# Row sizes of the last stores and the first loads where a streaming kernel goes from one half of its tokens to the next

## The chip, the core and the metric

The kernel runs on one core of a Trainium2 chip. The core has five engines with instruction streams of their own, and 16 DMA engines that carry data between the core's on-chip memory (SBUF, 128 partitions) and the device memory (HBM). The metric is the device time of one execution in microseconds (us). Before the change it is 242.05 us, the median of eight executions between 241.79 and 242.74 us.

## The reference

For each of 16 x 1024 tokens there is a row of 512 fp32 numbers and eight router logits. The two largest softmax weights, made to sum to one, scale two copies of the token's row:

```python
probs = softmax(router_logits)                       # (16, 1024, 8)
topk_indices = np.argsort(probs, axis=-1)[..., -k:]  # k = 2
topk_probs = np.take_along_axis(probs, topk_indices, axis=-1)
topk_probs = topk_probs / np.sum(topk_probs, axis=-1, keepdims=True)
return x[:, :, None, :].repeat(k, axis=2) * topk_probs[..., None]
```

The input is 33.6 MB and the output 67.1 MB. There are no matrix products. With two weights that sum to one, each of them is a sigmoid of the difference of the two largest logits.

## The kernel before

The 16384 tokens are laid over the 128 partitions, 128 consecutive tokens to each. A token is 2 KB of input and 4 KB of output, so in HBM a partition owns 256 KB of consecutive input and 512 KB of consecutive output. One DMA moves n tokens of every partition; it is cut into 128 rows, one per partition, and a row is n x 2 KB for a load and n x 4 KB for a store. Each row is one packet, and each of the 16 DMA engines carries eight of the 128.

First the logits are loaded (L72) and `top2_weights` works out `WA`, both weights of all tokens, on VectorE (DVE) and ScalarE (ACT). Then two groups of 64 tokens per partition follow (`GROUP = 64`, `M = 128`).

Two buffers hold the work. `xs` has room for the 64 input tokens of a group, 128 KB in each partition. `osp` has room for 16 output tokens, 64 KB. One DVE instruction (L99) multiplies n input tokens by their two weights and writes 2n rows. Which tokens go where is written out by hand in `plan`: tokens 0 to 15 go to `osp`, in pieces of 2 and 14. Tokens 16 to 31 go to `low`, the first half of `xs`, whose own input has been used by then. Tokens 32 to 47 go to `osp` again, in two pieces of 8. Tokens 48 to 63 go to `high`, the second half of `xs`, in two pieces of 8. Each piece is stored right after it is made (L107). So the second group's loads of tokens 0 to 31 must wait for the store from `low`, and its loads of 32 to 47 and of 48 to 63 for the first and the second store from `high`.

SP (SyncE) issues every DMA but one: the first store of the first group goes out on ACT's queue. SP issues in program order, and an issue that must wait holds back the later ones. The order is: logits, four loads of 16 tokens, the first group's stores, the second group's four loads (L96), the second group's stores. Once issued, the transfers of a queue are carried in the order of issue by each DMA engine. Eight completion semaphores are given out to the DMAs in turn, and an issue also waits until the DMA that had its semaphore before has landed.

Of the kernel before, what the change touches and what calls it, by code (L numbers as in the profile page):

```python
# [1 line left out]

# [4 lines left out]

F32 = mybir.dt.float32
ALU = mybir.AluOpType
ACTF = mybir.ActivationFunctionType  # L10
P = 128


def top2_weights(nc, pool, logits, M, E):

    hi, lo, n = None, None, E
    while n > 1:  # L20
        n //= 2
        if hi is None:
            a, b = logits[:, :, 0:n], logits[:, :, n : 2 * n]
            nhi = pool.tile([P, M, n], F32, tag=f"hi{n}")
            nlo = pool.tile([P, M, n], F32, tag=f"lo{n}")
            nc.vector.tensor_tensor(nhi, a, b, op=ALU.max)  # L26
            nc.vector.tensor_tensor(nlo, a, b, op=ALU.min)  # L27
        else:
            a, b = hi[:, :, 0:n], hi[:, :, n : 2 * n]
            nhi = pool.tile([P, M, n], F32, tag=f"hi{n}")  # L30
            nlo = pool.tile([P, M, n], F32, tag=f"lo{n}")
            tmp = pool.tile([P, M, n], F32, tag=f"tmp{n}")
            nc.vector.tensor_tensor(tmp, lo[:, :, 0:n], lo[:, :, n : 2 * n], op=ALU.max)  # L33
            nc.vector.tensor_tensor(nlo, a, b, op=ALU.min)  # L34
            nc.vector.tensor_tensor(nlo, nlo, tmp, op=ALU.max)  # L35
            nc.vector.tensor_tensor(nhi, a, b, op=ALU.max)  # L36
        hi, lo = nhi, nlo
    dlt = pool.tile([P, M], F32, tag="dlt")
    nc.vector.tensor_tensor(dlt, hi[:, :, 0], lo[:, :, 0], op=ALU.subtract)  # L39
    WA = pool.tile([P, M, 2], F32, tag="WA")  # L40
    nc.scalar.activation(WA[:, :, 0], dlt, ACTF.Sigmoid, scale=-1.0)  # L41
    nc.scalar.activation(WA[:, :, 1], dlt, ACTF.Sigmoid, scale=1.0)  # L42
    return WA


@with_exitstack
def kernel(
    ctx: ExitStack,
    tc: tile.TileContext,
    x: bass.AP,  # L50
    router_logits: bass.AP,
    k: bass.AP,
    out: bass.AP,
):
    nc = tc.nc
    B, S, D = x.shape
    E = router_logits.shape[-1]
    N = B * S
    assert int(k) == 2 and E == 8 and N % P == 0
    M = N // P  # L60

    GROUP = 64
    L = 16
    x_v = x.rearrange("b s d -> (b s) d").rearrange("(p m) d -> p m d", p=P)
    o_v = out.rearrange("b s k d -> (b s) k d").rearrange("(p m) k d -> p m k d", p=P)
    rl_v = router_logits.rearrange("b s e -> (b s) e").rearrange(
        "(p m) e -> p m e", p=P
    )

    wpool = ctx.enter_context(tc.tile_pool(name="wpool", bufs=1))  # L70
    logits = wpool.tile([P, M, E], F32)
    nc.sync.dma_start(logits, rl_v)  # L72
    WA = top2_weights(nc, wpool, logits, M, E)

    xs = wpool.tile([P, GROUP, D], F32)
    osp = wpool.tile([P, L, 2, D], F32)


    low = xs[:, : 2 * L, :].rearrange("p (r k) d -> p r k d", k=2)
    high = xs[:, 2 * L :, :].rearrange("p (r k) d -> p r k d", k=2)  # L80
    h = L // 2
    e = 2
    plan = [
        (0, e, osp[:, :e]),
        (e, L - e, osp[:, e:]),
        (L, L, low),
        (2 * L, h, osp[:, :h]),
        (2 * L + h, h, osp[:, h:]),
        (3 * L, h, high[:, :h]),
        (3 * L + h, h, high[:, h:]),  # L90
    ]

    for g in range(M // GROUP):
        m0 = g * GROUP
        for r in range(0, GROUP, L):
            nc.sync.dma_start(xs[:, r : r + L, :], x_v[:, m0 + r : m0 + r + L, :])  # L96
        for r, n, og in plan:
            rows = slice(m0 + r, m0 + r + n)
            nc.vector.tensor_tensor(  # L99
                og,  # L100
                xs[:, r : r + n, :].unsqueeze(2).to_broadcast([P, n, 2, D]),
                WA[:, rows, :].unsqueeze(3).to_broadcast([P, n, 2, D]),
                op=ALU.mult,
            )

            queue = nc.scalar if rows.start == 0 else nc.sync
            queue.dma_start(o_v[:, rows], og)  # L107


# [1 line left out]
_INS = ['x', 'router_logits', 'k']  # L111
_OUTS = [((16, 1024, 2, 512), 'float32')]

_NUMBERS = {'k': 2}


# [26 lines left out]
```

## Time and profile before

| | us |
|---|---|
| median of eight executions (lowest, highest) | 242.05 (241.79, 242.74) |
| the profiled execution, device time | 242.65 |
| its span on the core | 240.9 |
| outside its span | 1.75 |
| busy DVE | 142.1 |
| busy ACT | 1.8 |
| share of 16 DMA engines' span in use, SP's queue and ACT's | 97.5% and 1.0% |
| mean rate of the DMA engines | 420 GB/s |

The span runs from the first to the last instruction of the core. "Busy" of the DMA engines is the time that their packets took; a packet that is held up counts in full, so that a share near 100% can still hide lost time, and the rate must be read with it. The trace also holds the start, the duration and the size of each packet. The packets of one DMA engine follow each other without a gap, so the engine that carried a packet can be told from the ends and starts.

### The profile page before, as it was taken

How to read it: one execution, taken by the hardware profiler on the slowest of the kernel's cores; microseconds unless marked ns; L12 is line 12 of the kernel's file. 1: busy time of each engine (PE TensorE's matmuls, PEld its weight loads, DVE VectorE, ACT ScalarE, POOL GpSimd, SP SyncE). 2: the span in 40 equal slices, each digit the busy share in tenths (PEclk: the TensorE clock that was granted, in tenths of full speed). 3: DMA queues.
4: the chain of work that ended last, by engine and by line, in shares of the span. 5: the costliest groups of instructions: out<-in, count | busy, mean ns of one | idle time of the engine just before them, and what ended most of it. 6: DMA issues, size and time to landing. Idle time of an engine off the chain costs nothing.

```text
span 240.9 us, 116 instructions
## 1 busy us (share of the span) xinstructions
DVE 142.1 (59%) x25; ACT 1.8 (1%) x3; POOL 0.2 (0%) x4
## 2 busy tenths in 40 slices
DVE  2369999900499999200000999997007999990000
ACT  2000000000000000000000000000000000000000
POOL 0000000000000000000000000000000000000000
DMA  7999999997999999999999999999999999999995
GB/s 261 435 435 392 457 452 435 484 438 324 501 479 392 403 424 435 419 430 435 414 354 435 435 435 435 435 373 505 457 445 392 479 392 403 435 430 435 435 430 218
DMA packets 3312, 101.19 MB, mean 420 GB/s; under 512 B 368, under 2 KB 368, under 8 KB 496
## 3 DMA queue, kind: packets, MB, share of 16 engines
q1 hardware_dynamic: 3168, 100.14, 97.5%
q10 hardware_dynamic: 144, 1.05, 1.0%
HBM read 34.08 MB, written 67.11 MB: 420 GB/s over the span
## 4 chain that ended last, share of the span: by engine, by line
DMA 50%; DVE 32%; issue 7%; SPq 1%; DVEq 0%
DMA out_dram<-osp 26%; DMA xs<-in_x_dram 23%; DVE osp L99 18%; DVE xs L99 14%; SPq L96 0%; SPq L72 0%; SPq L107 0%; DVEq L99 0%
## 5 line engine op out<-in xcount | busy, mean ns | idle before, releaser
L99 DVE TENSOR_TENSOR osp<-xs,WA 128x8192 f32<-128x8192 f32 (+2 forms) x8 | 69.2, 8688 | 70.0 <-DMA xs<-in_x_dram 40.6
L99 DVE TENSOR_TENSOR xs<-xs,WA 128x8192 f32<-128x8192 f32 (+1 forms) x6 | 69.2, 11536 | 0.2
L26 DVE TENSOR_TENSOR nhi<-logits 128x512 f32<-128x512 f32 x1 | 0.7, 691 | 4.4 <-DMA logits<-in_router_logits_dram 4.4
L41 ACT ACT_TABLE_LOAD x1 | 1.3, 1283 | 0.7 <-PEq L124 0.7
L33 DVE TENSOR_TENSOR tmp<-nlo 128x256 f32<-128x256 f32 (+1 forms) x2 | 0.7, 351 | 0.0
L34 DVE TENSOR_TENSOR nlo<-nhi 128x256 f32<-128x256 f32 (+1 forms) x2 | 0.7, 350 | 0.0
L36 DVE TENSOR_TENSOR nhi<-nhi 128x256 f32<-128x256 f32 (+1 forms) x2 | 0.7, 350 | 0.0
L35 DVE TENSOR_TENSOR nlo<-nlo,tmp 128x256 f32<-128x256 f32 (+1 forms) x2 | 0.7, 349 | 0.0
L27 DVE TENSOR_TENSOR nlo<-logits 128x512 f32<-128x512 f32 x1 | 0.7, 684 | 0.0
L41 ACT ACTIVATE WA<-dlt 128x128 f32<-128x128 f32 x1 | 0.3, 315 | 6.2 <-DVE dlt L39 6.2
L39 DVE TENSOR_TENSOR dlt<-nhi,nlo 128x128 f32<-128x128 f32 x1 | 0.3, 291 | 0.0
L42 ACT ACTIVATE WA<-dlt 128x128 f32<-128x128 f32 x1 | 0.3, 299 | 0.0
L124 POOL MEMSET const-bfloat16-1.0<- 128x1 bf16 x1 | 0.1, 101 | 0.0
L124 POOL MEMSET const-uint8-127<- 128x1 uint8 x1 | 0.1, 101 | 0.0
L124 POOL MEMSET const-float32-0.0<- 128x1 f32 x1 | 0.1, 98 | 0.2 <-issue 0.2
L124 POOL MEMSET const-float32-1.0<- 128x1 f32 x1 | 0.1, 98 | 0.0
## 6 DMA issues: line engine op xcount, KB each, us to landing
xs<-in_x_dram SPq DMA_DIRECT2D x8, 4096.0 KB, 37.1
out_dram<-osp SPq DMA_DIRECT2D x4, 4096.0 KB, 20.7
out_dram<-xs SPq DMA_DIRECT2D x4, 4096.0 KB, 22.7
out_dram<-osp SPq DMA_DIRECT2D x2, 7168.0 KB, 31.8
out_dram<-osp ACTq DMA_DIRECT2D x1, 1024.0 KB, 16.4
out_dram<-osp SPq DMA_DIRECT2D x1, 1024.0 KB, 30.0
logits<-in_router_logits_dram SPq DMA_DIRECT2D x1, 512.0 KB, 3.7
out_dram<-xs SPq DMA_DIRECT2D x2, 33.9
```

Source lines behind the costliest of these rows:

```text
L26: nc.vector.tensor_tensor(nhi, a, b, op=ALU.max)
L27: nc.vector.tensor_tensor(nlo, a, b, op=ALU.min)
L33: nc.vector.tensor_tensor(tmp, lo[:, :, 0:n], lo[:, :, n : 2 * n], op=ALU.max)
L34: nc.vector.tensor_tensor(nlo, a, b, op=ALU.min)
L35: nc.vector.tensor_tensor(nlo, nlo, tmp, op=ALU.max)
L36: nc.vector.tensor_tensor(nhi, a, b, op=ALU.max)
L39: nc.vector.tensor_tensor(dlt, hi[:, :, 0], lo[:, :, 0], op=ALU.subtract)
L41: nc.scalar.activation(WA[:, :, 0], dlt, ACTF.Sigmoid, scale=-1.0)
L42: nc.scalar.activation(WA[:, :, 1], dlt, ACTF.Sigmoid, scale=1.0)
L99: nc.vector.tensor_tensor(og, xs[:, r : r + n, :].unsqueeze(2).to_broadcast([P, n, 2, D]), WA[:, rows, :].unsqueeze(3).to_broadcast([P, n, ...
L124: nc = _bacc.Bacc("TRN2", target_bir_lowering=False, num_devices=1)
```

## The change

The second group's first load of 16 tokens becomes four loads of 2, 2, 4 and 8 tokens, with rows of 4, 4, 8 and 16 KB instead of one row of 32 KB. In both groups the last piece of 8 tokens (56 to 63) becomes two pieces of 4 with a DVE instruction and a store each, with rows of 16 KB instead of 32 KB. In the second group the first 16 tokens are no longer made in pieces of 2 and 14 but in one piece, stored with rows of 64 KB. The first group's loads and its pieces of 2 and 14 stay as they were.

```diff
+LOADS = [[16] * 4, [2, 2, 4, 8] + [16] * 3]
 ...
+    begin = [[(0, e, osp[:, :e]), (e, L - e, osp[:, e:])], [(0, L, osp)]]
     plan = [
-        (0, e, osp[:, :e]),
-        (e, L - e, osp[:, e:]),
         (L, L, low),
         (2 * L, h, osp[:, :h]),
         (2 * L + h, h, osp[:, h:]),
         (3 * L, h, high[:, :h]),
-        (3 * L + h, h, high[:, h:]),
+        (3 * L + h, h // 2, high[:, h : h + h // 2]),
+        (3 * L + h + h // 2, h // 2, high[:, h + h // 2 :]),
     ]
 
     for g in range(M // GROUP):
         m0 = g * GROUP
-        for r in range(0, GROUP, L):
-            nc.sync.dma_start(xs[:, r : r + L, :], x_v[:, m0 + r : m0 + r + L, :])
-        for r, n, og in plan:
+        r = 0
+        for n in LOADS[g]:
+            nc.sync.dma_start(xs[:, r : r + n, :], x_v[:, m0 + r : m0 + r + n, :])
+            r += n
+        for r, n, og in begin[g] + plan:
```

## The prediction

> **What bounds the kernel now.** I read the page's slices and queues first.
>
> ```profile
> DMA  7999999997999999999999999999999999999995
> GB/s 261 435 435 392 457 452 435 484 438 324 501 479 392 403 424 435 419 430 435 414 354 435 435 435 435 435 373 505 457 445 392 479 392 403 435 430 435 435 430 218
> q1 hardware_dynamic: 3168, 100.14, 97.5%
> q10 hardware_dynamic: 144, 1.05, 1.0%
> ```
>
> The DMA engines are in use for 98.5% of the span, DVE for 59%: the DMAs are the bound. The usual rate is 435 GB/s (slices that hold packets of over 32 KB scatter, since a packet counts where it starts). 101.19 MB at 435 GB/s is 232.6 us of the 240.9. Below the usual rate with 32 KB packets on both sides lie slice 20 (120 to 126 us, 354) and slice 26 (157 to 163 us, 373). Next I read the waits, DVE's and then SP's, and the order in time around slice 20.
>
> ```profile
> DVE osp L99 <- DMA xs<-in_x_dram: 40.6, 2, 34.6
> DVE osp L99 <- DMA out_dram<-osp: 29.4, 2, 14.8
> ...
> SPq L96 <- DMA out_dram<-xs: 21.9, 2, 11.0
> ```
>
> ```profile
> 98.12 0.33 SPq L107 DMA_DIRECT2D out_dram<-xs  x1
> 98.50 24.70 SPq L96 DMA_DIRECT2D xs<-in_x_dram  x4
> 132.71 17.29 DVE L99 TENSOR_TENSOR osp<-xs,WA 128x2048 f32<-128x2048 f32 x2 [34.62 <-DMA xs<-in_x_dram]
> 135.03 15.35 SPq L107 DMA_DIRECT2D out_dram<-osp  x2
> 150.04 17.22 DVE L99 TENSOR_TENSOR xs<-xs,WA 128x16384 f32<-128x16384 f32 x1
> ```
>
> DVE waits 40.6 us for loads and 29.4 us for stores, always behind a full queue: the first group's last store is issued at 98.12 us and two loads by 100.5, although those loads begin to move at 121. So the loss in slice 20 isn't a queue that ran empty. The view by stages, in three stretches of 29 us, shows stores alone, the change from stores to loads, and loads alone (columns: DVE, ACT, POOL busy, clock, DMA share, GB/s):
>
> ```profile
> 72.20:101.27 29.07, 25.82 (x3) 0.00 (x0) 0.00 (x0) 1.00 0.99 427
> 101.27:130.34 29.07, 0.00 (x0) 0.00 (x0) 0.00 (x0) 1.00 1.00 414
> 130.34:159.41 29.07, 26.67 (x3) 0.00 (x0) 0.00 (x0) 1.00 1.01 431
> ```
>
> The share stays at 1.00 while the rate falls: packets are held up. The packet records give the size of it. A 32 KB packet takes 1.211 us in either direction, 8 KB 0.309, 4 KB 0.159, 56 KB 2.116, 64 KB 2.418 and a completion mark 0.009. Time above these, as a mean over the 16 engines:
>
> ```
>    0 to 10 us   first reads (4 KB, 0.84 to 1.14 us each)            0.82 us
>   17 to 25 us   8 KB stores of ACT's queue among 32 KB loads        0.56
>  118 to 121 us  last store packets before the loads (about 1.89)    0.71
>  121 to 126 us  first load packets after the stores (about 1.33)    0.59
>  156 to 162 us  last load packets before the stores                 0.54
>  whole span                                                         3.44
> ```
>
> So the change from stores to loads costs 0.71 + 0.59 = 1.30 us, and that is what the edit can touch. The engines' last packets end at 238.5 us in the mean, but the slowest at 239.65; it sets the end.
>
> **The change part by part.** A 16 KB packet by interpolation between 8 and 32 KB: 0.309 + (1.211 - 0.309) / 3 = 0.610 us.
>
> *Packets.* Each DMA engine carries eight rows of each DMA. The first load of the second group now takes 16 x 0.159 + 8 x 0.309 + 8 x 0.610 + 4 x 0.009 = 9.93 us for 8 x 1.211 + 0.009 = 9.70: +0.23. Each split store takes 16 x 0.610 + 0.018 = 9.78 for 9.70: +0.08, twice: +0.16. The merged first store takes 8 x 2.418 + 0.009 = 19.35 for 8 x (0.309 + 2.116) + 0.018 = 19.42: -0.07. Sum +0.33 us, on the path in full, since the DMA engines are the bound.
>
> *The switch from stores to loads.* No row shows it with small rows. From below, all of it goes (-1.30). From above, nothing goes, or it grows as in the first rival. The nearest row is the stretch from 17 to 25 us, where eight 8 KB stores per engine alternate with 32 KB loads: 0.56 us for eight alternations, 0.07 each, against 1.30 for one switch with 32 KB on both sides. It is not the same thing (two queues), but it speaks for a loss that goes with the size of what is in flight. The last store packet is already held up in the engine that reaches it first, before any engine could have finished its stores: the loads' reads start while it is still being written. If what is read ahead is counted in packets, the store part halves with 16 KB rows (0.36) and the load part falls to an eighth with 4 KB rows (0.07). I take 0.43 us, between 0.07 and 1.30: -0.87.
>
> *The switch from loads to stores.* Its first store rows go from 8 to 64 KB. Bounds: no change, since the time is lost in the last load packets, which stay at 32 KB; or as much as the other switch, 1.30 for 0.54 (+0.76). I take 0, because the store packets after this switch show no time above their usual one; the upper end is a rival. A gain is bounded by all of it, -0.54.
>
> *DVE.* One instruction more in the first group, none more in the second. Two 128x8192 instructions of 8.69 us become two pairs; a 128x2048 takes 2.29 us and a 128x14336 15.08, together 17.37 against 17.22 for one 128x16384, so a cut costs about 0.15. The last piece would be ready at 98.3 instead of 98.1 us, with stores queued until 111, and at the end at 217.0 instead of 216.8, with stores queued until 228.8 on the mean engine: nothing. In the second group the one piece of 16 tokens waits for all four loads, which land as late as the one did plus 0.23 (about 132), and gives its store to SP at about 149.5 to 150. Before, the store of 2 tokens was issued at 135 and of 14 at 150.03. Loads cover this until 161.4: nothing. If that cover were gone, the queue would stand for up to 15 us.
>
> *SP's queue.* One store issue more in each group (0.33 us each), three load issues more (0.33 to 0.99 us each), one store issue less. The semaphores given out in turn make the load of 8 tokens wait for the store of tokens 32 to 39 (landed at 92) and the load of 16 to 31 wait for that of 40 to 47 (landed at 101.9), where it was issued at 99.5 before. Behind it stand only the loads of 32 to 47 and 48 to 63, which wait for stores from `high` anyway (111.6 and 122.9). The queue holds work until 121 and then the small loads until 131: nothing. The longest price if a wait fell in the open is 2.4 us.
>
> *A rule against it.* In the trace a completion mark between two transfers takes 0.009 us, and no gap follows it. The Trainium skill, "DMA: Bandwidth & Descriptors", section "Measured (HBM→SBUF, 128 partitions, SWDGE, issued from GpSimd)", says to batch DMAs to at least 1 MiB for at least 75% of the peak; the two loads of 2 tokens have 512 KB each. By that rule these two would run at 75% of 435 GB/s, 3.2 us for 2.4, and the sum would be 0.8 us worse. The rows here show transfers queued without a gap, so I do not take it.
>
> *Sum.* +0.33 - 0.87 = -0.54 us. The profiled execution took 242.65 us (240.9 of span, 1.75 outside), 0.6 over the median; the slowest engine's lag of 1.1 us is the likely reason. Against the execution the sum gives 242.1, against the median **241.5 us**.
>
> **The rivals.**
>
> *Short reads run dry* (the other side). 4 KB reads keep less under way. At the start the first ones took up to 1.14 us and the later ones followed every 0.159, so about seven were in flight. At the switch reads may come later: the last store landed 1.2 us after its last packet, where 0.3 is usual. If a read then takes 0.84 + 0.9 = 1.7 us with seven in flight, a 4 KB packet takes 0.24 instead of 0.159, and sixteen of them lose 1.3 us. With the store part at 0.36 the switch costs 1.70 for 1.30: +0.40 + 0.33, 242.8 us. It decides for slower by over 0.2% (0.48 us) when the 4 KB packets lose 1.1 us in all, 0.07 each. Against it: at the start they ran at 0.159.
>
> *The loss belongs to the change of direction, not to the rows.* Then the edit doesn't do what it says: +0.33, 242.4 us. For it: both switches lose the time in the last packet of the old direction, as a fixed latency would.
>
> *Large first store rows widen the other switch.* 0.54 becomes 1.30: 242.3 us with my gain at the first switch, 243.1 without it.
>
> **How the numbers follow.** Two kernels of this kind can be told apart from about 0.2% (0.48 us). Forecast, the loss shrinks with the rows: 0.50, its own range 240.9 to 242.0 (from 0.0 to 0.9 left at the switch, with 0.2 of scatter in the slowest engine); 0.38 of it faster, 0.12 the same. Direction alone: 0.18, of it 0.12 the same and 0.06 slower. Short reads: 0.17, slower. The other switch: 0.15, of it 0.06 the same, 0.09 slower. Together 0.38, 0.30, 0.32. The range for eight in ten reaches from 240.9 to 242.9, past the price of the short reads.
>
> **What would show it.** In the changed profile, slice 20 should come above 354 GB/s, and packets at 118 to 126 us should lose about 0.4 us instead of 1.30; 4 KB packets near 0.159 us speak against short reads, 0.24 for them; about 0.54 lost at 156 to 162 speaks against the third rival; DVE should idle before the second group's first piece as long as before. Any slice of DMA share under 9 at 98 to 165 us would say that a cover which I cost at nothing is gone. I am wrong if the bytes in flight, not the packets, set the loss.

## The result, and the profile after

The changed kernel takes 241.39 us (median of 12 executions, 241.17 to 241.77), the kernel before 242.05 us beside it (32 executions). The ratio is 0.9971 with a 95% interval of 0.9964 to 0.9979: 0.66 us less by the medians. The forecast was 241.5 us.

The page of the changed kernel, with its span, slices and queues:

```profile
span 239.9 us, 121 instructions
...
DMA  7999999979989899999999999999999898999996
GB/s 262 437 437 393 454 388 432 525 344 459 503 350 525 350 437 437 437 437 396 434 372 459 437 437 437 437 437 415 459 393 481 383 492 350 437 437 437 437 413 287
...
q1 hardware_dynamic: 3744, 100.14, 97.8%
q10 hardware_dynamic: 144, 1.05, 1.0%
```

Slice 20, which holds the change from stores to loads, went from 354 to 372 GB/s, and slice 26, with the change back, from 373 to 437 (slice 27 has 415 now). SP's queue has 576 packets more, which is what the cuts put in. From 98 us to 165 us no slice of the share is under 9. Its waits of DVE and of SP, and the order in time around the switch:

```profile
DVE osp L105 <- DMA xs<-in_x_dram: 39.7, 2, 33.7
DVE osp L105 <- DMA out_dram<-osp: 29.2, 2, 14.9
...
SPq L101 <- DMA out_dram<-xs: 18.9, 2, 10.6
```

```profile
98.44 0.33 SPq L113 DMA_DIRECT2D out_dram<-xs  x1
98.82 24.17 SPq L101 DMA_DIRECT2D xs<-in_x_dram  x7
132.09 17.23 DVE L105 TENSOR_TENSOR osp<-xs,WA 128x16384 f32<-128x16384 f32 x1 [33.68 <-DMA xs<-in_x_dram]
149.34 0.34 SPq L113 DMA_DIRECT2D out_dram<-osp  x1
149.35 17.22 DVE L105 TENSOR_TENSOR xs<-xs,WA 128x16384 f32<-128x16384 f32 x1
```

DVE starts the second group at 132.09 instead of 132.71 us, and its first store is issued at 149.34, when loads still have to come until 161. So the waits only moved; the gain is in the DMA engines. The same stretches as before, stores alone, the switch, loads alone (columns: DVE, ACT, POOL busy, clock, DMA share, GB/s):

```profile
72.20:101.27 29.07, 26.10 (x4) 0.00 (x0) 0.00 (x0) 1.00 1.00 434
101.27:130.34 29.07, 0.00 (x0) 0.00 (x0) 0.00 (x0) 1.00 1.01 420
130.34:159.41 29.07, 27.29 (x2) 0.00 (x0) 0.00 (x0) 1.00 1.02 434
```

The middle stretch rose from 414 to 420 GB/s. A stretch counts a packet where it starts, so such a rate is known to a few GB/s only; the sizes below are from the packet records, as the time of packets above their usual one, a mean over the 16 engines. The kernel before was profiled once more among the experiments, in an execution of 241.97 us. That shows what belongs to the kernel and what to one execution. Its page has in slice 20 the same dip:

```profile
GB/s 262 437 437 393 458 431 426 518 344 420 502 349 524 349 437 437 437 437 437 437 349 437 437 437 437 437 342 533 401 382 524 349 524 349 437 437 437 437 437 262
```

```
us above the usual packet times     before   before,   changed
                                             again
stores to loads (116 to 130 us)      1.31     1.28      0.71
  of it in the last store packets    0.71     0.69      0.44
  of it in the first load packets    0.59     0.58      0.25
loads to stores (153 to 166 us)      0.55     0.57      0.32
ACT's stores among loads (15 to 27)  0.56     0.60      0.80
usual packet times, summed         233.97   233.97    234.31
mean end of the 16 engines         238.53   238.56    238.16
end of the slowest engine          239.65   238.99    238.55
device time of the execution       242.65   241.97    241.64
```

(The two parts of the first row stop at 126 us or less and so add up to slightly less than it.) From the second column to the third, the packets cost 0.34 us more, the switch from stores to loads costs 0.57 less, the switch back 0.25 less and the stretch with ACT's stores 0.20 more. That is -0.28; the mean end moved by -0.40. Most of the other 0.12 lies in the way of counting. In every trace here a packet starts 3 to 4 ns before the one ahead of it on its engine has ended, so a sum of durations counts that little twice. Each engine carries 36 packets more in the changed kernel, which makes 0.13 us. In time the cuts therefore cost about 0.2 us and not 0.34. By the same correction a split store costs about 0.05 us (16 + 2 packets for 8 + 1) where its durations say 0.08, and the cut load about 0.13 where they say 0.23.

### The profile page after: what moved, and what is told of

It is laid out like the page before. It is cut to its first block, busy times and chain, and to the rows that moved or that the text cites. A ratio compares the mean times of both kernels' runs of the same rounds, so it can differ in the third digit from the quotient of the medians.

```text
span 239.9 us, 121 instructions
## 1 busy us (share of the span) xinstructions
DVE 142.4 (59%) x26; ACT 1.8 (1%) x3; POOL 0.2 (0%) x4
## 4 chain that ended last, share of the span: by engine, by line
DMA 45%; DVE 36%; issue 7%; SPq 1%; DVEq 0%
DMA out_dram<-osp 26%; DVE osp L105 22%; DMA xs<-in_x_dram 18%; DVE xs L105 15%; SPq L101 1%; SPq L76 0%; SPq L113 0%; DVEq L105 0%
## 5 line engine op out<-in xcount | busy, mean ns | idle before, releaser
L105 DVE TENSOR_TENSOR osp<-xs,WA 128x8192 f32<-128x8192 f32 (+3 forms) x7 | 69.1, 9908 | 68.9 <-DMA xs<-in_x_dram 39.7
L105 DVE TENSOR_TENSOR xs<-xs,WA 128x4096 f32<-128x4096 f32 (+2 forms) x8 | 69.5, 8691 | 0.3
```

Of the source, the lines that this page charges most:

```text
L105: nc.vector.tensor_tensor(og, xs[:, r : r + n, :].unsqueeze(2).to_broadcast([P, n, 2, D]), WA[:, rows, :].unsqueeze(3).to_broadcast([P, n, ...
```

## The experiments

Three theories were set against each other, in the short names that the expectations use. Theory 1 is the forecast's: the last stores' rows set the store part of the loss, the first loads' rows the load part. Theory 2: only the first loads' rows count, through what is read ahead while stores are still being written. Theory 3: only the last stores' rows count. Every ratio is to the kernel before on the same chip. The diffs write each group's list of pieces out in full, as they stand in the kernel before or in the run that is named.

**The loads alone.** Diff against the kernel before, which has 16 tokens in each load:

```diff
-LOADS = [[16] * 4, [16] * 4]
+LOADS = [[16] * 4, [2, 2, 4, 8] + [16] * 3]
```

> The kernel before with the second group's first load alone cut into 2, 2, 4 and 8 tokens; stores as before. Packets cost +0.23 us. Theory 1 (as predicted: each side's own rows set its own part of the loss): the store part of the switch stays at 0.71 us, the load part falls from 0.59 to about 0.1, net about -0.25: 241.8 us. Theory 2 (what counts is how much the first loads read ahead while stores are still being written): the switch falls as far as in the changed kernel, from 1.30 to about 0.65 us, net -0.4: 241.65 us. Theory 3 (only the last stores' rows count): the switch stays at 1.30, 242.3 us.

Measured: 241.88 us, ratio 0.9994 (0.9985 to 1.0003), no difference that can be told. The packet records show 0.65 us in the last store packets and 0.34 in the first load packets. The store part stayed, which speaks against theory 2, and the load part fell by 0.25. The packets' cost, 0.23 by durations and about 0.13 in time, eats up half of that or all of it. So the cut of the loads acts where the forecast had it act, on the load part, but its gain is too small to be seen in the time.

**The last stores alone.** In the first group, against the kernel before:

```diff
-        (3 * L + h, h, high[:, h:]),
+        (3 * L + h, 4, high[:, h : h + 4]),
+        (3 * L + h + 4, 4, high[:, h + 4 :]),
```

> The kernel before with the first group's last store alone cut into two of 4 tokens; loads as before. Packets cost +0.08 us. Theory 1: the store part falls from 0.71 to 0.36 us, net -0.27: 241.8 us. Theory 2: the switch stays at 1.30, 242.1 us. Theory 3: the switch falls to about 0.65, net -0.57: 241.5 us.

Measured: 241.52 us, ratio 0.9971 (0.9960 to 0.9983), as much as the whole change. The store part is 0.43 us and the load part 0.33, although the loads have 32 KB rows as before. The middle one of the three stretches:

```profile
101.27:130.34 29.07, 0.00 (x0) 0.00 (x0) 0.00 (x0) 1.00 1.00 422
```

It has 422 GB/s for the 414 of the kernel before. So small last stores also shorten the load part. That is more than theory 1 said and close to theory 3, which put 0.65 at the switch where the records have 0.77.

**The first store of the second group alone.** In the second group, against the kernel before:

```diff
-        (0, e, osp[:, :e]),
-        (e, L - e, osp[:, e:]),
+        (0, L, osp),
```

> The kernel before with the second group's pieces of 2 and 14 tokens alone merged into one of 16. Packets gain 0.07 us. If the smaller loss at the switch from loads to stores in the changed kernel's profile (0.30 for 0.54 us) is the merger's doing, net -0.31: 241.75 us. If it is scatter of single profiles, net -0.07: 242.0 us. If large first store rows widen that switch, up to +0.7: 242.7 us.

Measured: 242.14 us, ratio 0.9997 (0.9988 to 1.0006). The switch from loads to stores cost 0.63 us with 64 KB first store rows, against 0.55 and 0.57 with 8 KB rows. By themselves they neither help nor hurt, so the merger alone doesn't explain the smaller loss there in the changed kernel. Whether it has a part in it beside the cut loads, this run can't say.

**Without the cut at the very end.** In the second group, against the changed kernel:

```diff
-        (3 * L + h, h // 2, high[:, h : h + h // 2]),
-        (3 * L + h + h // 2, h // 2, high[:, h + h // 2 :]),
+        (3 * L + h, h, high[:, h:]),
```

> The changed kernel without the split of the second group's last store, behind which no loads stand. By all three theories only its packets count: 0.08 us less than the changed kernel, 241.3 us. If smaller last rows let the slowest engine end earlier, it is slower than the changed kernel by up to 0.3 us: 241.7.

Measured: 241.25 us, ratio 0.9958 (0.9944 to 0.9971). The interval touches that of the changed kernel, so the 0.14 us between the medians is not shown; the direction is that of the packets.

**Larger last stores.** The dose the other way, in the first group, with loads as before:

```diff
-        (3 * L, h, high[:, :h]),
-        (3 * L + h, h, high[:, h:]),
+        (3 * L, L, high),
```

> The kernel before with the first group's last two stores of 8 tokens merged into one of 16, rows of 64 KB; loads as before. Packets gain 0.08 us. If the store part of the loss goes with the last stores' rows (0.48 us measured with 16 KB, 0.71 with 32 KB), it rises to 1.1 to 1.4: net +0.3 to +0.6, 242.4 to 242.7 us. If 32 KB is already the most that counts, 242.0.

Measured: 242.50 us, ratio 1.0013 (1.0005 to 1.0022), slower with fewer packets. The store part rose to 0.97 us. The same three stretches of this kernel's profile:

```profile
72.20:101.27 29.07, 25.56 (x2) 0.00 (x0) 0.00 (x0) 1.00 1.00 433
101.27:130.34 29.07, 0.00 (x0) 0.00 (x0) 0.00 (x0) 1.00 0.98 399
130.34:159.41 29.07, 26.87 (x3) 0.00 (x0) 0.00 (x0) 1.00 1.01 432
```

Stores and loads alone run as fast as ever; the stretch with the switch has 399 GB/s where the kernel before has 414. The loss grows with the rows, but less than in proportion: 0.97 for 64 KB, 0.71 for 32.

**Finer last stores.** Diff against the kernel without the cut at the end, first group:

```diff
         (3 * L, h, high[:, :h]),
-        (3 * L + h, 4, high[:, h : h + 4]),
-        (3 * L + h + 4, 4, high[:, h + 4 :]),
+        (3 * L + h, 4, high[:, h : h + 4]),
+        (3 * L + h + 4, 2, high[:, h + 4 : h + 6]),
+        (3 * L + h + 6, 2, high[:, h + 6 :]),
```

> The changed kernel without the cut at the very end (241.25 us measured), with the first group's last pieces 4, 2, 2 instead of 4, 4 tokens, so that the last two stores have 8 KB rows. Packets cost about +0.09 us. If the store part goes on falling with the rows (0.44 us in that kernel), it loses another 0.15 to 0.2: net -0.1, 241.15 us. If a fixed part of about 0.45 is left, 241.35 us.

Measured: 240.83 us, ratio 0.9947 (0.9935 to 0.9959), the fastest of all; its interval lies clear of the changed kernel's, but not of that of the kernel without the cut at the end (0.9944 to 0.9971), from which it differs by the finer stores alone. The store part is 0.07 us and the load part 0.11. The page and the three stretches of this kernel:

```profile
span 238.9 us, 122 instructions
...
GB/s 280 422 439 395 439 417 439 443 413 461 505 351 527 351 439 439 428 417 406 421 414 459 439 439 439 428 450 461 417 439 439 417 461 357 433 439 439 439 439 263
```

```profile
72.20:101.27 29.07, 26.18 (x5) 0.00 (x0) 0.00 (x0) 1.00 0.99 429
101.27:130.34 29.07, 0.00 (x0) 0.00 (x0) 0.00 (x0) 1.00 1.00 422
130.34:159.41 29.07, 27.79 (x2) 0.00 (x0) 0.00 (x0) 1.00 1.01 436
```

Slice 20 has 414 GB/s and hardly dips. The loss at the switch is gone but for 0.18 us, and the switch back lost 0.04 in this profile. No fixed loss of the change from stores to loads is left that would be worth naming.

**Small last loads.** Diff against the kernel without the cut at the end:

```diff
-LOADS = [[16] * 4, [2, 2, 4, 8] + [16] * 3]
+LOADS = [[16] * 4, [2, 2, 4, 8] + [16] * 2 + [8, 4, 2, 2]]
```

> The changed kernel without the cut at the very end (241.25 us measured), with the second group's last load cut into 8, 4, 2 and 2 tokens ahead of the first store, the mirror of the edit. Packets cost +0.23 us. If the loss at the switch from loads to stores (0.37 us in that kernel) goes with the rows of the last loads, it falls to about 0.1: 241.2 us. If not, 241.5 us.

Measured: 241.38 us, ratio 0.9966 (0.9954 to 0.9978). The switch from loads to stores lost 0.14 us for 0.37, and the time shows no gain. That the smaller last loads took the difference isn't shown: the kernel with the finer stores has 32 KB last loads and lost 0.04 there.

**The same cut away from the switch.** Diff against the kernel before:

```diff
-LOADS = [[16] * 4, [16] * 4]
+LOADS = [[16] * 4, [16, 16] + [2, 2, 4, 8] + [16]]
```

> The kernel before with the third load of the second group cut into 2, 2, 4 and 8 tokens, in the middle of the loads, where no switch is. If the packets' cost is as worked out, +0.23: 242.3 us, and no part of the 1.30 us goes. If small rows help anywhere, for example by bringing the 16 engines into step, 242.0 us or less.

Measured: 241.88 us, ratio 0.9987 (0.9979 to 0.9996): faster by 0.24 us, where 0.23 more had been expected for the packets. The switch from stores to loads kept its loss (1.41 us), so the cut acts on that one only where it stands at it. But the switch back, 20 us later, lost 0.15 us instead of 0.55 to 0.57. This was a miss; what follows from it stands with the hardware below.

**Finer last stores with the first load in one piece.** Diff against the kernel with the finer last stores:

```diff
-LOADS = [[16] * 4, [2, 2, 4, 8] + [16] * 3]
+LOADS = [[16] * 4, [16] * 4]
```

> The kernel with 8 KB rows in the last two stores (240.83 us measured), but with the second group's first load in one piece again, rows of 32 KB. Packets gain 0.23 us. If each side's rows set its own part, the load part comes back (about 0.3 with small last stores): 240.9 us. If what counts is only that the last stores are small, 240.6 us. If the slowest engine's lag and the other switch were helped by the small loads (they were 0.35 and 0.04 us there, 1.1 and 0.55 in the kernel before), up to 241.5 us.

Measured: 241.25 us, ratio 0.9960 (0.9948 to 0.9973). At the switch 0.31 us are lost (0.20 in stores, 0.10 in loads), 0.13 more than with the cut loads; the switch back lost 0.50 us, 0.46 more. Less what the uncut load saves (0.23 by durations, about 0.13 in time), that is +0.36 to +0.46. The medians differ by 0.42 and the ratios by 0.31 us, but their intervals overlap. So with small last stores the cut loads do little for the switch that they stand at. The middle stretch has

```profile
101.27:130.34 29.07, 0.00 (x0) 0.00 (x0) 0.00 (x0) 1.00 1.01 431
```

431 GB/s, more than the 422 with cut loads, although more is lost in it. That is how far such a rate can be trusted for one profile, and why the losses are taken from the packet records.

**Only one store of small rows.** Diff against the kernel with the finer last stores, first group:

```diff
-        (3 * L, h, high[:, :h]),
-        (3 * L + h, 4, high[:, h : h + 4]),
-        (3 * L + h + 4, 2, high[:, h + 4 : h + 6]),
-        (3 * L + h + 6, 2, high[:, h + 6 :]),
+        (3 * L, 14, high[:, :14]),
+        (3 * L + 14, 2, high[:, 14:]),
```

> The kernel with 8 KB rows in the last two stores (240.83 us measured), but with the first group's last pieces 14 and 2 tokens instead of 8, 4, 2, 2: rows of 56 KB and then one store of 8 KB rows. Packets gain 0.18 us. If only the rows of the very last store count, the switch stays at about 0.2 us: 240.65 us. If one store of 8 KB rows (2.5 us) isn't enough after large rows, the store part comes back by up to 0.7: 241.3 us.

Measured: 241.04 us, ratio 0.9953 (0.9939 to 0.9966). The time can't be told from that of the finer stores, but the profile shows where the packets' gain went. The stretch with the switch:

```profile
101.27:130.34 29.07, 0.00 (x0) 0.00 (x0) 0.00 (x0) 1.00 0.98 405
```

It has 405 GB/s against 422, with a store part of 0.45 and a load part of 0.38 us, together 0.65 us more than with the finer stores (17 GB/s would be 1.2 us, so the rate overstates it). By this one profile it isn't the rows of the very last store alone that count; those more than 2.5 us ahead of the loads, which that store takes, count too.

**The first group's first store on SP's queue.** In the first group, against the kernel with the finer last stores:

```diff
-        (0, e, osp[:, :e]),
-        (e, L - e, osp[:, e:]),
+        (0, L, osp),
-            queue = nc.scalar if rows.start == 0 else nc.sync
-            queue.dma_start(o_v[:, rows], og)
+            nc.sync.dma_start(o_v[:, rows], og)
```

> The kernel with 8 KB rows in the last two stores (240.83 us measured), with the first group's first 16 tokens made and stored in one piece on SP's queue, so that no stores alternate with the loads at 17 to 25 us. Packets gain 0.07 us, and the loss of that stretch (0.6 to 0.8 us in the profiles) goes; one switch from loads to stores takes its place at 46 us, which costs 0.04 to 0.67 us in the profiles. Expected 240.3 us; if that switch costs as much as the alternation, 240.8 us.

Measured: 241.15 us, ratio 0.9963 (0.9950 to 0.9976): not faster, a miss. The alternation's 0.72 us went (0.02 left), but the switch from loads to stores that took its place lost 1.18 us at 39 to 43 us. The stretches around it, first this kernel:

```profile
30.00:36.00 6.00, 5.97 (x2) 0.00 (x0) 0.00 (x0) 1.00 1.01 437
36.00:42.00 6.00, 6.00 (x1) 0.00 (x0) 0.00 (x0) 1.00 1.03 382
42.00:48.00 6.00, 6.00 (x1) 0.00 (x0) 0.00 (x0) 1.00 0.98 404
```

At 36 to 48 us the rate falls to 382 and 404 GB/s. The first switch of this kind costs more than any of the second (0.04 to 0.67 us); why is not settled.

**The kernel before once more.**

> The kernel before itself, for a second trace. If the losses at the switches belong to the kernel, the switch from stores to loads again costs about 1.3 us and that from loads to stores about 0.55, 242.1 us; what differs from the first trace is the scatter of single profiles, and the slowest engine's lag (1.1 us there) is the first suspect.

Measured: 241.97 us. The losses at the two switches came back as 1.28 and 0.57 us, and the mean end of the engines as 238.56 us after 238.53. Only the slowest engine differed, 238.99 for 239.65, and that is the 0.68 us between the two executions.

The store and load parts of all these profiles in one table, in us:

```
last store rows   first load rows   store part   load part
64 KB             32 KB                0.97        0.64
32 KB             32 KB           0.69 to 0.71   0.58 to 0.69   (before, twice; two others)
32 KB              4 KB                0.65        0.34         (loads alone)
16 KB             32 KB                0.43        0.33         (stores alone)
16 KB              4 KB           0.37 to 0.44   0.20 to 0.25   (changed kernel; two others)
 8 KB             32 KB                0.20        0.10
 8 KB              4 KB           0.04 to 0.07   0.11 to 0.23   (finer stores; that on SP's queue)
 8 KB after 56 KB  4 KB                0.45        0.38
```

## Why the prediction was right, step by step

*What bounds the kernel.* Right. DVE's waits shrank by under a microsecond and SP's wait for stores by 3, since SP comes to it later (the last load issue ahead of its first long wait, the fifth, ends at 103.3 us, where the second ended at 100.5); both end behind a full queue as before, and what changed the time was time of the DMA engines' packets.

*Packets, +0.33 us.* Right as a sum of durations: the usual packet times sum to 234.31 us after 233.97, and a 16 KB packet took 0.611 us for the interpolated 0.610. But the term was put "on the path in full", and in time it is about 0.2 us, since each packet starts 3 to 4 ns before the one ahead has ended and there are 36 more of them on each engine. It was 0.13 us too large.

*The switch from stores to loads, 0.43 us left, a gain of 0.87.* The mechanism was right and the size was off: 0.71 us is left, a gain of 0.57 to 0.60. The store part was put at half (0.36) and is 0.44; the load part was put at an eighth (0.07) and is 0.25. The term that was mis-sized most is the load part, for which the loads' own rows were taken as the only measure. They count (0.34 for 0.59 us with the loads alone), but the last stores' rows count as much or more: with 8 KB stores the load part is 0.10 even with 32 KB loads. The picture behind it, that loads reading ahead in whole packets hold the last stores up, fell with the loads alone: an eighth of the load row left 0.65 of 0.71 us of the store part. The sign of being wrong that the prediction named, a loss set by the bytes in flight whatever the rows, did not come: with the same 32 KB loads the loss is 1.62, 1.3, 0.77 and 0.31 us for last store rows of 64, 32, 16 and 8 KB.

*The switch from loads to stores, taken as unchanged.* It lost 0.25 us less in the changed kernel, so this term was too cautious and made up for the one before. The bound below had allowed a gain. Neither the merged store alone (0.63 us) nor the cut loads alone (0.64) show it; the changed kernel has both (0.32). Its cause is open, so this part of the gain is luck as far as the forecast goes.

*The sum.* -0.54 was forecast; the medians moved by -0.66 (by the ratio's interval, 0.51 to 0.87 us). The gain at the first switch was put 0.27 to 0.30 too high, that at the second 0.25 too low and the packets' cost 0.13 too high. That these errors nearly cancel is luck; the forecast's direction and the first switch as the main term are not.

*DVE and SP at nothing.* Right: no slice between 98 and 165 us shows an empty queue, though the load of tokens 16 to 31 was issued only at 102.4 us, 0.4 us after the earlier store named in the prediction had landed.

*The slowest engine.* The profiled execution's 0.6 us over the median were put down to its slowest engine. The second profile shows that: the mean end is the same, the slowest one is not.

*Rivals.* Short reads run dry: no, the 256 packets of 4 KB lost 0.012 us each in the mean, and 0.018 in the worst microsecond, against 0.07 needed. The loss belongs to the direction: no, 0.18 us of 1.30 are left with 8 KB stores. Large first store rows: not at the second group's switch (0.63 for 0.55 to 0.57); the first group's switch with 64 KB rows did lose 1.18 us, in a kernel other than the one forecast.

*The rule on 1 MiB per DMA*, of the Trainium skill, "DMA: Bandwidth & Descriptors", section "Measured (HBM→SBUF, 128 partitions, SWDGE, issued from GpSimd)", differs from the trace here, and the measurement decides. Its figures are for DMAs issued from GpSimd; the loads here are issued by SP, with other work queued around them. Seven in ten of the 4 KB packets of the two 512 KB loads took the usual 0.159 us (up to 0.165), and a completion mark 0.009, with no gap behind it. The prediction took the rule as 75% for these loads; it gives that for 1 MiB, so its price of 0.8 us was an estimate from below.

## What to carry to other kernels

Where one queue goes from stores to loads, look at the packets around the switch, not at the share of busy time, which stays at 100% while packets are held up. Cut the last stores before the switch to rows of 16 and then 8 KB, a few microseconds of them. Against it count about 0.05 us for each split of eight rows per engine into sixteen, and the overlap of packets when durations are summed. Test the parts of such an edit one by one: here the cut of the last stores alone gives as much as the whole change (0.9971 both), and the form with finer stores (240.83 us), which also has the cut loads and the merged store, beats both kernels.

## What the runs showed of the hardware

The time lost when the DMA engines go from stores to loads depends mostly on the rows of the last stores: 1.62 us in all with 64 KB, 1.3 with 32, 0.77 with 16 and 0.31 with 8, each with 32 KB loads behind, and the times go the same way (242.50, 242.05, 241.52 and 241.25 us, the last with the merged store as well). What happens inside an engine then is not shown by these runs. One sign can be left aside: in the kernel before, the last store lands 1.27 us after its completion mark, where 0.37 is usual, but with the finer stores it still lands 0.86 us after it while nearly all of the loss is gone, so a late landing by itself isn't what costs the time.

With cut loads in the second group the later switch from loads to stores mostly lost less, even with the cut 20 us away from it. Seven of the eight profiles with cut loads show 0.04 to 0.41 us there, the six without 0.50 to 0.67; the one against it is that of the loads alone, with 0.64. But six of those seven also have the merged store of 64 KB rows behind that switch. Uncut loads with that store lost 0.63 and 0.50, so neither part alone explains the six; in the seventh, the cut away from the first switch, 0.15 was lost without the merger. With one profile for most kernels, the cause stays open.

The slowest of the 16 engines ended 0.3 to 1.1 us after their mean, and in two executions of the same kernel the time differed by just this. A change of half a microsecond is therefore to be read from the mean over the engines in a profile, and from many executions in the time.
